# A hybrid encoder layer on one core: its 32 experts from split weight pairs and 64-token halves to float32 throughout, in units of 64 and 32 tokens

## The chip, the cores and the metric

One core of a Trainium2 chip runs the whole layer in one launch. The metric is device time in microseconds (us) of one execution. In what follows PE is TensorE, ACT ScalarE, DVE VectorE, POOL GpSimd and SP SyncE; SP and POOL here mostly issue DMAs.

## The reference

1024 tokens of width 1024 pass a token mixer (mLSTM heads and a spatial gating unit), cross-attention into 256 memory tokens, a mixture of experts, and a final RMSNorm, all in float32. The change lies in the experts:

```python
g_idx    = top_k(softmax(h @ w_rg + b_rg), 1)        # 1 of 4 groups
e_top    = top_k(e_logits of that group, 2)          # 2 of its 8 experts
weights  = p_top * softmax(e_top)
# for each of the 32 experts e, over the tokens that chose it:
y        = (silu(xb @ w_gate[e]) * (xb @ w_up[e])) @ w_down[e]   # 1024 -> 512 -> 1024
out[t]  += weight * y                                 # each token has two experts
x        = x + out;  result = rms_norm(x, g_final)
```

2048 pairs of token and expert fall on 32 experts very unevenly, and which expert gets how many is known only on the device. Every expert's weights are 6 MB.

## The kernel before

The expert stage follows the cross-attention. The hidden rows `h` (normed) and the residual `acc` lie in device memory; a table in device memory (`tab_dram`) holds for every expert its tokens and their weights. The stage walks through blocks, one per expert and a second one for the fullest, in the order of the string `ORDER` (line 42). Four experts are fixed and go first; the others are ranked by their number of tokens on the device (`assign`, line 1254, run in the middle of the first block), and the string says which rank stands where. W is a block of up to 128 tokens, N one of up to 64, T the second block of the fullest expert. Tokens that find no place are done by a loop at the end (line 1487) that runs as often as needed; in the profiled execution it ran no trip.

**Weights.** An expert's weights come as six DMAs of 1 MB on SP's queue (`load`, line 918: four for gate and up, two for down), each into one of `SEATS` = 16 raw buffers of 128 x 2048. `prep_r` issues loads up to the number of free seats; `free` (line 1406) is called when a chunk has been used for the last time and lets it go on. Eleven loads go out before the stage.

**W blocks.** `weights` (line 1156) splits a raw chunk with ACT (cast to the high part, line 108) and DVE (the rest as the low part, line 109) into buffers `wh` and `wl`, four of each; the raw buffer is free once it is split. `mm3` (lines 99 to 102) then does three matmuls in the format f32r for each product, with 128 tokens as stationary and 512 columns moving. `prep_w` (line 1398) runs the splits three chunks ahead of the matmuls (`LA`).

**N and T blocks.** The raw chunk itself is the moving operand, in float32. 64 tokens are the stationary operand, once for the left half and once for the right half of the array's columns, and the two halves get different columns of the weights (`gu_part_n` line 1186, `dn_part_n` line 1225). The trace shows each such float32 matmul as two records. The raw buffer is free when PE has used it. Two N blocks share one gathered tile of 128 tokens.

Each block gathers its tokens from `h` by an indirect DMA on POOL, two blocks ahead (line 1434); PE transposes them (`transpose_x`, line 1414), and SiLU and product are done by ACT and DVE. The down matmuls of block b - 1 run after the gate and up matmuls of block b, and in the midst of the latter `turned` transposes the former's activations.

**Results.** ACT scales each row by its weight, and POOL issues an indirect DMA that adds to `acc`: for a W block 128 whole rows of 4 KB (`store`, line 1236), for an N block 128 half rows of 2 KB (`store_n`, line 1244), since an N block's result lies as left halves on the first 64 partitions and right halves on the others. The final norm reads `acc` afterwards.

```python
LA = 3
for i in range(4):                       # gate and up chunks of block b
    gu_part(...) if wide else gu_part_n(...)
    if not wide: free(b, i)              # narrow: seat free after PE
    done += 1
    prep_w(done + LA)                    # wide: split, seat free after DVE
```

Of the kernel before, what the change touches and what calls it, by code (L numbers as in the profile page):

```python
# [18 lines left out]
P = 128  # L19
# [23 lines left out]
ORDER = "WWWW" + "NNN" + "WN" * 4 + "TWN" + "WN" * 3 + "WWNWWNWNN"  # L43
NS = ORDER.count("N")
SEATS = 16
# [3 lines left out]
def tile_hybrid_encoder(ctx: ExitStack, tc: tile.TileContext,  # L49
# [42 lines left out]
    tab_dram = tc.dram_tile([P * 256, 2], I32, name="tab_dram")  # L92
# [291 lines left out]
    with tpool(name="work1b", bufs=2, side="right") as work, \  # L384
            tpool(name="gmath", bufs=1, side="right") as gm:
        tab0 = gm.tile([P, 256, 2], I32, name="tab0")
        nc.gpsimd.memset(tab0, 0)
        nc.gpsimd.iota(tab0[:, :, 0], pattern=[[0, 256]], base=S, channel_multiplier=1)
        nc.scalar.dma_start(tab_dram.rearrange("(p c) k -> p c k", c=256), tab0)
# [432 lines left out]
    nc.gpsimd.iota(cidx, pattern=[[1, NU]], base=0, channel_multiplier=NU, allow_small_or_imprecise_dtypes=True)  # L822
# [3 lines left out]
    nc.gpsimd.memset(kcol[:, 2:3], 0.0)  # L826
    nc.gpsimd.memset(kcol[64:128, 2:3], 1.0)
# [61 lines left out]
    for k in ORDER:  # L889
        n = sum(b[0] == "W" for b in blocks)  # L890
        if k == "W":
            tw = ORDER[:len(blocks)].count("T")
            blocks.append(("W", ("e", n) if n < FIXED else
                           ("r", 0 if ORDER[len(blocks) - 1] == "T" else n - FIXED + 1 - tw)))
        elif k == "T":
            blocks.append(("N", ("t", 0)))
        else:
            blocks.append(("N", ("r", NL + sum(b[0] == "N" and b[1][0] == "r" for b in blocks))))
# [4 lines left out]
    assert NB == NE + 1 and len(narrow) == NS + 1 and len(narrow) % 2 == 0 and blocks[twin + 1][1] == ("r", 0)  # L903
    seq = []
# [137 lines left out]
    def route_s(t, c, alone=False):  # L1042
# [16 lines left out]
        V.tensor_scalar(bi, bi, 6, None, op0=ALU.logical_shift_right)  # L1059
        bf = small([P, 2], "bf")  # L1060
        V.tensor_copy(bf, bi)
        V.tensor_scalar(pos, pos, 512.0, None, op0=ALU.mult)
        V.scalar_tensor_tensor(pos, eid, 16.0, pos, op0=ALU.mult, op1=ALU.add)
        dst = small([P, 2], "dst", I32)
        V.scalar_tensor_tensor(dst, bf, -32767.0, pos, op0=ALU.mult, op1=ALU.add)
# [73 lines left out]
    with ExitStack() as pa:  # L1139
        rawp[2] = pa.enter_context(tpool(name="raw5", bufs=SEATS - 11))  # L1140
        whp = pa.enter_context(tpool(name="wh7", bufs=4))
        wlp = pa.enter_context(tpool(name="wl7", bufs=4))
        mc = pa.enter_context(tpool(name="mc", bufs=1))
        pgu = pa.enter_context(tpool(name="pgu", bufs=4, space=PSUM))
        xHL = pp.tile([P, KT, P], F32R, name="xH"), pp.tile([P, KT, P], F32R, name="xL")
        ybuf = [pp.tile([P, KT, P], F32R, name=n).rearrange("p a b -> p (a b)").bitcast(F32) for n in ("xH", "xL")]
        xgs += [pp.tile([P, D], F32, name="x1t"), mc.tile([P, D], F32, name="xg")]
        sgt = mc.tile([P, 512], F32, name="sg")
        mHL = mc.tile([P, 4, P], F32R, name="mH"), mc.tile([P, 4, P], F32R, name="mL")
        xTn = mc.tile([P, KT, P], F32, name="xTn")  # L1150
        sgn = sgt[:, 0:256]
        mTn = mc.tile([P, 2, P], F32, name="mTn")
        cnts = {"g": 0, "y": 0}
        acc2 = acc.rearrange("s (h d) -> (s h) d", h=2)

        def weights(r):
            hl = []
            for k in range(2):
                h = whp.tile([P, 1024], F32R, name="wh")
                l = wlp.tile([P, 1024], F32R, name="wl")  # L1160
                split(h, l, r[:, k * 1024:(k + 1) * 1024])
                hl.append((h.rearrange("p (b c) -> p b c", b=2), l.rearrange("p (b c) -> p b c", b=2)))
            return hl
# [4 lines left out]

        def xpose(xg):
            return transposed(xg, trt, xHL)  # L1170

        def xpose_n(xg):
            for g in range(2):
                tp = trt()
# [30 lines left out]
        def mpose(sg):  # L1205
            tp = trt()
            for j in range(4):
                nc.tensor.transpose(tp[:, j], sg[:, j * P:(j + 1) * P], ident)
# [376 lines left out]
```

## Time and profile before

| | us |
|---|---|
| median of 3 runs (lowest, highest) | 1385.25 (1385.24, 1386.29) |
| the profiled execution, whole | 1385.45 |
| the profiled execution, span from first to last instruction | 1383.7 |
| first weight load issued in the expert stage | 774.2 |
| first matmul of an expert | 803.3 |
| end of the last matmul of an expert | 1350.2 |
| final norm, to the end | 1383.7 |

The mean granted TensorE clock was 0.971 of full speed. The page gives busy times per engine over the whole span; a stage has its own mix, so the stretches of the expert stage are read apart. "DMA share" is the mean busy share of the core's 16 DMA engines; a busy engine is no bound unless something waits for it.

### The profile page before, as it was taken

What the parts mean: (1) busy time and instruction counts of PE and PEld (TensorE: products, weight loads), DVE (VectorE), ACT (ScalarE), POOL (GpSimd) and SP (SyncE); (2) the same over time, 40 slices, a digit from 0 to 9 for tenths busy, and PEclk for the clock granted to TensorE, in tenths of its full rate; (3) what the DMA queues carried; (4) which work ended last, traced back from release to release, by engine and by line L of the source; (5) the groups of instructions that cost most, each with busy time, mean ns of one, the idle gap of its engine ahead of it and who ended that gap; (6) DMA issues with size and microseconds to landing.
All of it is one profiled execution on the core that took longest, in us unless ns stands there. A gap on an engine that the chain in (4) does not pass through costs nothing. (4 is left out here: it accounts for less than half of the span.)

```text
span 1383.7 us, 18356 instructions
## 1 busy us (share of the span) xinstructions
PE 1271.4 (92%) x6505; PEld 970.5 (70%) x6505; DVE 793.1 (57%) x1532; ACT 612.9 (44%) x1043; POOL 188.3 (14%) x283
## 2 busy tenths in 40 slices
PE   6899999999897899999999679999999999999980
PEld 6899888888886788888888557655555555566530
DVE  5643465883477765753467668645546454667512
ACT  7632343331474442653222248545446454556522
POOL 2000100000021111110133221112111111100012
PEclk9999999999999999999999879999999999999995
DMA  8820122311798652543963568999999999999967
GB/s 317 267 74 1 36 80 84 92 38 42 236 310 283 215 187 100 199 141 108 338 248 112 213 223 313 388 399 402 399 393 395 392 377 391 378 386 379 384 230 265
DMA packets 86750, 339.53 MB, mean 245 GB/s; under 512 B 12008, under 2 KB 24488, under 8 KB 62081
## 3 DMA queue, kind: packets, MB, share of 16 engines
q1 hardware_dynamic: 72672, 304.53, 59.0%
q0 software_dynamic: 11536, 26.31, 6.6%
q10 hardware_dynamic: 2448, 7.51, 1.4%
q8 instruction: 52, 0.85, 0.3%
q14 instruction: 42, 0.34, 0.1%
HBM read 297.06 MB, written 50.67 MB: 251 GB/s over the span
## 5 line engine op out<-in xcount | busy, mean ns | idle before, releaser
L109 DVE TENSOR_TENSOR wl<-wraw,wh 128x1024 fp32r<-128x1024 f32 (+2 forms) x276 | 325.2, 1210 | 118.2 <-ACT wh L108 106.5
L108 ACT CAST wh<-wraw 128x1024 fp32r<-128x1024 f32 (+2 forms) x276 | 277.7, 1037 | 97.4 <-PE mm L101 29.8
L1191 PE MATMUL gu<-wraw,xTn 128*64 128x512 f32 x512 | 118.2, 598 | 0.5 <-DMA wraw<-in_w_gu_dram 0.5
L101 PE MATMUL gu<-wl,xH 128*128 128x512 f32 x272 | 109.4, 402 | 1.3 <-DVE wl L109 1.1
L102 PE MATMUL gu<-wh,xL 128*128 128x512 f32 x272 | 107.6, 396 | 0.0
L100 PE MATMUL gu<-wh,xH 128*128 128x512 f32 x272 | 99.3, 405 | 2.4 <-ACT wh L108 1.7
L100 PE MATMUL mm<-hH,wh 128*128 128x512 f32 x256 | 100.3, 392 | 0.8 <-ACT wh L108 0.8
L101 PE MATMUL mm<-hL,wh 128*128 128x512 f32 x256 | 100.2, 391 | 0.0
L102 PE MATMUL mm<-hH,wl 128*128 128x512 f32 x256 | 100.0, 391 | 0.0
L1191 PEld LDWEIGHTS gu<-wraw,xTn 128*64 128x64 f32 x512 | 34.2, 136 | 63.8 <-issue 59.7
L108 ACT CAST xH<-tp 128x512 fp32r<-128x512 f32 x64 | 35.4, 589 | 67.7 <-PE tp L738 67.4
L101 PEld LDWEIGHTS gu<-wl,xH 128*128 128x128 f32 x272 | 52.2, 192 | 16.9 <-DVE wl L109 5.7
L100 PEld LDWEIGHTS gu<-wh,xH 128*128 128x128 f32 x272 | 51.9, 191 | 17.2 <-ACT wh L108 4.4
L101 PE MATMUL mm<-wl,hH 128*128 128x384 f32 (+2 forms) x192 | 61.7, 321 | 0.0
L102 PE MATMUL mm<-wh,hL 128*128 128x384 f32 (+2 forms) x192 | 61.6, 321 | 0.0
L100 PE MATMUL mm<-wh,hH 128*128 128x384 f32 (+2 forms) x192 | 61.3, 319 | 0.0
L1228 PE MATMUL y<-wraw,mTn 128*64 128x512 f32 x256 | 60.2, 602 | 1.1 <-ACT mTn L1216 1.1
L101 PE MATMUL y<-wl,mH 128*128 128x512 f32 x136 | 56.3, 414 | 5.2 <-DVE wl L109 5.2
L102 PEld LDWEIGHTS gu<-wh,xL 128*128 128x128 f32 x272 | 51.9, 191 | 11.4 <-DVE xL L109 0.2
L109 DVE TENSOR_TENSOR xL<-tp,xH 128x512 fp32r<-128x512 f32 x64 | 42.7, 685 | 23.7 <-ACT xH L108 23.5
L100 PEld LDWEIGHTS mm<-hH,wh 128*128 128x128 f32 x256 | 48.1, 188 | 10.7 <-ACT wh L108 1.1
L102 PEld LDWEIGHTS mm<-hH,wl 128*128 128x128 f32 x256 | 48.1, 188 | 10.2 <-issue 0.2
(418 smaller groups left out, 2730.5 us busy)
## 6 DMA issues: line engine op xcount, KB each, us to landing
wraw<-in_w_gu_dram SPq DMA_DIRECT2D x128, 1024.0 KB, 22.5
wraw<-in_w_dn_dram SPq DMA_DIRECT2D x64, 1024.0 KB, 23.3
wraw<-in_w_kv_dram SPq DMA_DIRECT2D x16, 512.0 KB, 5.2
xt<-in_x_dram SPq DMA_DIRECT2D x16, 512.0 KB, 5.8
wraw<-in_w_cm_dram SPq DMA_DIRECT2D x16, 512.0 KB, 3.7
x1t<-x_dram SPq DMA_DIRECT2D x16, 512.0 KB, 3.9
wraw<-in_w_tm_dram SPq DMA_DIRECT2D x8, 520.0 KB, 5.3
wraw<-in_w_qT_dram SPq DMA_DIRECT2D x8, 512.0 KB, 7.1
```

The source lines that it names most:

```text
L100: nc.tensor.matmul(o, ah, bh, start=first, stop=False)
L101: nc.tensor.matmul(o, ah, bl, start=False, stop=False)
L102: nc.tensor.matmul(o, al, bh, start=False, stop=last)
L108: nc.scalar.copy(h, r)
L109: nc.vector.tensor_tensor(l, r, f32(h), op=ALU.subtract)
L1191: nc.tensor.matmul(ps[q * 64:q * 64 + 64].rearrange("p (b c) -> p b c", b=2), xT[:, kt, hf * 64:hf * 64 + 64], r4[:, k, :, q * 256:q * 256 ...
L1228: nc.tensor.matmul(ps[q * 64:q * 64 + 64], mT[:, k, i * 64:i * 64 + 64], r[:, k * 1024 + q * 512:k * 1024 + q * 512 + 512], start=i == 0 a ...
```

## The change

All blocks run in float32 from the raw chunks; `weights`, `prep_w`, the buffers `wh` and `wl` and the three-matmul products of the experts are gone. `SEATS` is 20, the four more in the space of those buffers, and every raw buffer is free when PE has used it. The string has new letters: A (15 blocks) is a unit of 64 tokens on column halves, as in N, and a unit of 32 tokens on column quarters: the 32 are stationary four times, and each quarter of the array's columns gets its own 256 columns of the chunk. B (2 blocks) is two units of 64. N and T (16) stay units of 64. `turn` lets the two units of a block swap places from chunk to chunk. Results leave as whole rows for all blocks: ACT copies a 64-unit's two halves (64 x 512 each), DVE a second unit's halves or quarters, onto one tile, DVE scales that tile's rows, and one indirect DMA adds 64, 96 or 128 rows. The table of tokens is cut into units of 32 instead of 64; the rows of the fullest expert's second block come by four small DMAs instead of two; the reads of the ranked order stand ahead of each expert's loads, where ten stood together.

```diff
-ORDER = "WWWW" + "NNN" + "WN" * 4 + "TWN" + "WN" * 3 + "WWNWWNWNN"
+ORDER = "AAAA" + "NNN" + "AN" * 4 + "TBN" + "BN" + "AN" * 2 + "AANAANANN"
-SEATS = 16
+SEATS = 20
...
+    def parts(b):
+        return {"A": [(64, 0, 0), (32, 64, 64)], "B": [(64, 0, 0), (64, 64, 64)],
+                "N": [(64, 64 * half_of[b][1] if b in half_of else 0, 0)]}[...]
...
-        whp = pa.enter_context(tpool(name="wh7", bufs=4))
-        wlp = pa.enter_context(tpool(name="wl7", bufs=4))
...
+        def turn(us, i):
+            us = list(enumerate(us))
+            return us[::-1] if i % 2 else us
+
+        def gu_part(pss, us, xT, r, i):
             r4 = r.rearrange("p (a b c) -> p a b c", a=2, b=2)
+            for u, (n, c0, _) in turn(us, i):
+                w = 4 * n
+                for k in range(2):
+                    kt = 2 * i + k
+                    for q in range(P // n):
+                        nc.tensor.matmul(pss[u][q * n:q * n + n].rearrange("p (b c) -> p b c", b=2),
+                                         xT[:, kt, c0:c0 + n], r4[:, k, :, q * w:q * w + w],
+                                         start=kt == 0, stop=kt == KT - 1)
...
+        def store(pss, us, tok, wt):
             cnts["y"] += 1
+            y = ybuf[cnts["y"] % 2]
+            for u, (n, _, o) in enumerate(us):
+                w = 8 * n
+                for q in range(P // n):
+                    (nc.vector.tensor_copy if u else nc.scalar.copy)(y[o:o + n, q * w:q * w + w], pss[u][q * n:q * n + n])
+            n = us[-1][2] + us[-1][0]
+            nc.vector.tensor_scalar(y[0:n], y[0:n], wt[0:n], None, op0=ALU.mult)
+            nc.gpsimd.indirect_dma_start(out=acc, out_offset=bass.IndirectOffsetOnAxis(ap=tok[0:n], axis=0),
+                                         in_=y[0:n], in_offset=None, bounds_check=S - 1, oob_is_err=False,
+                                         compute_op=ALU.add)
...
                 for i in range(4):
-                    if wide:
-                        gu_part(ps, xx[b], ws[b, i], i)
-                    else:
-                        gu_part_n(ps, xx[b], half_of[b][1], ws[b, i], i)
-                    if not wide:
-                        free(b, i)
-                    done += 1
-                    prep_w(done + LA)
+                    gu_part(ps, us, xx[b], raw(b, i), i)
+                    free(b, i)
```

SP's order at the start of the expert stage, before: five loads (`DMAHW` and `PE` are the semaphores of earlier DMAs and of PE), then six that wait for the splits on ACT and DVE, then the reads of the ranked order.

```order
L920 DMA wraw<-in_w_gu_dram 128x2048 [waits DMAHW1_49,PE_49]
L920 DMA wraw<-in_w_gu_dram 128x2048
L920 DMA wraw<-in_w_gu_dram 128x2048 [waits DMAHW5_49,PE_49]
L922 DMA wraw<-in_w_dn_dram 128x2048 [waits DMAHW6_49]
L922 DMA wraw<-in_w_dn_dram 128x2048 [waits DMAHW7_49]
L920 DMA wraw<-in_w_gu_dram 128x2048 [waits DMAHW0_49,DVE_49,Activation_49]
L920 DMA wraw<-in_w_gu_dram 128x2048 [waits DMAHW1_49,DVE_49,Activation_49]
L920 DMA wraw<-in_w_gu_dram 128x2048 [waits DMAHW2_49,DVE_49]
L920 DMA wraw<-in_w_gu_dram 128x2048 [waits DMAHW3_49,DVE_49]
L922 DMA wraw<-in_w_dn_dram 128x2048 [waits DMAHW4_49,DVE_49]
L922 DMA wraw<-in_w_dn_dram 128x2048 [waits DMAHW5_49,DVE_49]
L1373 TENSOR_LOAD perm [waits DVE_49]
```

The same place with the change, from the first load of the stage on: nine loads that wait for earlier DMAs or for PE of the stage before, then two that wait for PE's use of the first chunks, and then the reads, one ahead of an expert's loads.

```order
L926 DMA wraw<-in_w_gu_dram 128x2048 [waits DMAHW3_49,PE_49]
L926 DMA wraw<-in_w_gu_dram 128x2048 [waits DMAHW4_49]
L926 DMA wraw<-in_w_gu_dram 128x2048 [waits DMAHW5_49,PE_49]
L928 DMA wraw<-in_w_dn_dram 128x2048 [waits DMAHW6_49]
L928 DMA wraw<-in_w_dn_dram 128x2048 [waits DMAHW7_49]
L926 DMA wraw<-in_w_gu_dram 128x2048 [waits DMAHW0_49]
L926 DMA wraw<-in_w_gu_dram 128x2048 [waits DMAHW1_49,PE_49]
L926 DMA wraw<-in_w_gu_dram 128x2048 [waits DMAHW2_49]
L926 DMA wraw<-in_w_gu_dram 128x2048 [waits DMAHW3_49]
L928 DMA wraw<-in_w_dn_dram 128x2048 [waits DMAHW4_49,PE_49]
L928 DMA wraw<-in_w_dn_dram 128x2048 [waits DMAHW5_49,PE_49]
L1349 TENSOR_LOAD perm [waits DVE_49]
```

What moved: the waits for DVE and ACT are gone from the loads, four more loads stand ahead of the first one that needs a used chunk, and that one now waits for PE.

PE's order in the gate and up part of a wide block, before (`gu` is the result in PSUM, `xH` and `xL` the halves of the tokens, `sg` the activations of the block before):

```order
L101 MATMUL gu<-wl,xH 128x512
L102 MATMUL gu<-wh,xL 128x512
L1208 MATMUL tp<-ident,sg 128x128 x4
L100 MATMUL gu<-wh,xH 128x512
L101 MATMUL gu<-wl,xH 128x512
L102 MATMUL gu<-wh,xL 128x512
L100 MATMUL gu<-wh,xH 128x512
```

A block of the kind A with the change (`gh`, `yh` are results of the 64-unit, `gq`, `yq` of the 32-unit; `wraw` is the moving operand, the shape is that of one result: tokens x columns):

```order
L1189 MATMUL gh<-wraw,xH 64x512 x4
L1189 MATMUL gq<-wraw,xH 32x256 x16
L1189 MATMUL gh<-wraw,xH 64x512 x4
L1207 MATMUL tp<-ident,sg 128x128 x3
L1189 MATMUL gh<-wraw,xH 64x512 x4
L1189 MATMUL gq<-wraw,xH 32x256 x16
L1189 MATMUL gh<-wraw,xH 64x512 x4
L1165 MATMUL tp<-ident,xg 128x128 x8
L1222 MATMUL yh<-wraw,mT_7588 64x512 x4
L1222 MATMUL yq<-wraw,mT_7589 32x256 x16
L1222 MATMUL yh<-wraw,mT_7588 64x512 x4
L1189 MATMUL gh<-wraw,xL 64x512 x4
```

What moved: three records of 128 x 512 for each product have become 64 x 512 in pairs and 32 x 256 in fours, and the two units alternate with a change of shape in the middle of each chunk.

ACT's last instructions of the stage, before (`mTn` are the last activations, `xH` and `xL` here the tiles of results):

```order
L1239 ACTIVATE xL<-y,wtw 128x512 x2
L1201 ACTIVATE sg<-gu 128x256
L1246 ACTIVATE xH<-y,wtn 128x512
L1216 COPY mTn<-tp 128x256
L1246 ACTIVATE xL<-y,wtn 128x512
```

The same with the change:

```order
L1198 ACTIVATE sg<-gh 128x256
L1231 COPY xH<-yh 64x512 x2
L1210 COPY mT_7588<-tp 128x256
L1464 DMA gfb<-in_g_final_dram 128x1024
L1231 COPY xL<-yh 64x512 x2
```

What moved: the last result takes two copies on ACT where there was one scaling, and a scaling of 64 x 1024 on DVE follows them.

## Rows read from the trace of the kernel before

**Rows 1.** The page's part 1: busy time of each engine, its share of the span, instructions.
```profile
PE 1271.4 (92%) x6505; PEld 970.5 (70%) x6505; DVE 793.1 (57%) x1532; ACT 612.9 (44%) x1043; POOL 188.3 (14%) x283
```

**Rows 2.** The expert stage cut into stretches (windows view): start and end in us, length, then busy us and instructions of PE, PEld, DVE, ACT and POOL, the granted TensorE clock, the share of the 16 DMA engines' time, GB/s.
```profile
774.00:790.00 16.00, 8.65 (x51) 6.63 (x50) 11.23 (x55) 6.75 (x13) 1.65 (x4) 0.84 0.91 341
790.00:810.00 20.00, 10.61 (x43) 8.53 (x42) 13.75 (x42) 4.80 (x8) 8.24 (x9) 0.62 0.51 176
810.00:820.00 10.00, 5.88 (x27) 4.51 (x26) 9.08 (x24) 7.02 (x7) 2.62 (x2) 0.95 0.97 364
820.00:850.00 30.00, 28.65 (x125) 23.30 (x126) 22.72 (x43) 19.04 (x23) 3.96 (x3) 0.85 0.68 237
...
880.00:1325.00 445.00, 423.73 (x1903) 249.16 (x1902) 232.19 (x240) 223.82 (x289) 63.30 (x45) 0.99 1.01 390
1325.00:1330.00 5.00, 4.96 (x12) 3.39 (x11) 4.09 (x4) 2.26 (x3) 0.00 (x0) 0.50 1.00 416
1330.00:1340.00 10.00, 10.00 (x45) 4.64 (x44) 0.00 (x0) 1.27 (x2) 1.56 (x1) 0.95 0.42 146
1340.00:1346.00 6.00, 4.46 (x22) 1.26 (x18) 0.42 (x1) 0.89 (x2) 0.00 (x0) 1.00 0.15 46
```

**Rows 3.** The DMA view of the stretch 880 to 1325 us: the two queues with packets, MB and share of the 16 engines (q1 holds the weight loads, q0 gathers and stores of tokens), and the weight loads issued there, KB each, median us from issue to landing.
```profile
q1 hardware_dynamic: 21973, 160.03, 89.1%
q0 software_dynamic: 6624, 13.22, 12.1%
...
wraw<-in_w_gu_dram SPq DMA_DIRECT2D x100, 1024.0 KB, 23.3
wraw<-in_w_dn_dram SPq DMA_DIRECT2D x54, 1024.0 KB, 23.6
```

**Rows 4.** What SP, the engine that issues the weight loads, waited for from 770 us on (waits view): line and what released it, us in total, times, longest us.
```profile
SPq L920 <- DMA wraw<-in_w_gu_dram: 113.4, 48, 4.7
SPq L920 <- DMA wraw<-in_w_dn_dram: 101.1, 42, 4.3
...
SPq L920 <- DVE wl L109: 53.3, 17, 14.4
```

**Rows 5.** SP's timeline around the start of the expert stage and at its last loads: start, length of the piece, line, operation, count.
```profile
774.24 6.04 SPq L920 DMA_DIRECT2D wraw<-in_w_gu_dram  x3
780.33 0.90 SPq L922 DMA_DIRECT2D wraw<-in_w_dn_dram  x2
795.65 17.13 SPq L920 DMA_DIRECT2D wraw<-in_w_gu_dram  x4
815.51 4.54 SPq L922 DMA_DIRECT2D wraw<-in_w_dn_dram  x2
...
1315.98 8.87 SPq L922 DMA_DIRECT2D wraw<-in_w_dn_dram  x4
```

**Rows 6.** PE's timeline (PE is the matmuls, PEld the loading of their weights): the first expert matmul, the gap at the ordering of experts, eight transposes and the 24 matmul records of a wide block's down part that follow them, a transpose between matmuls of 64 columns, two waits near the end, a 64-token gate/up part and the last down part. In brackets the idle time ahead and what ended it.
```profile
803.31 0.79 PE L100 MATMUL gu<-wh,xH 128*128 128x512 f32 x1
...
820.17 0.26 PE L1275 MATMUL tp<-MT,kcol 32*1 32x32 f32 x2 [4.29 <-DVE t L1340]
...
838.98 1.03 PE L738 MATMUL tp<-ident,xg 128*128 128x128 f32 x8
839.77 0.48 PE L100 MATMUL y<-wh,mH 128*128 128x512 f32 x1
...
845.31 0.39 PE L100 MATMUL gu<-wh,xH 128*128 128x512 f32 x1
...
1312.00 0.33 PE L1208 MATMUL tp<-ident,sg 128*128 128x128 f32 x1
...
1312.26 1.94 PE L1228 MATMUL y<-wraw,mTn 128*64 128x512 f32 x8
...
1322.63 0.44 PE L1215 MATMUL tp<-ident,sg 128*128 128x128 f32 x2 [0.94 <-DVE sg L1202]
...
1324.48 1.22 PE L100 MATMUL y<-wh,mH 128*128 128x512 f32 x2 [1.41 <-ACT wh L108]
...
1333.35 7.09 PE L1191 MATMUL gu<-wraw,xTn 128*64 128x512 f32 x32
...
1333.83 0.14 PEld L1191 LDWEIGHTS gu<-wraw,xTn 128*64 128x64 f32 x2 [0.29 <-issue]
...
1346.50 3.65 PE L1228 MATMUL y<-wraw,mTn 128*64 128x512 f32 x16 [1.10 <-ACT mTn L1216]
```

**Rows 7.** The timeline after the last matmul: ACT's scaling of the last result, POOL's issue of the last store.
```profile
1350.25 0.69 ACT L1246 ACTIVATE xL<-y,wtn 128x512 f32<-128x512 f32 x1 [3.80 <-issue]
1351.82 1.56 POOL L1247 DMA_INDIRECT acc<-xL,tk  x1 [3.80 <-ACTq L1486]
```

**Rows 8.** Groups of instructions from 700 us on, shapes apart (lines view): busy us and mean ns of one, then idle time ahead.
```profile
L109 DVE TENSOR_TENSOR wl<-wraw,wh 128x1024 fp32r<-128x1024 f32 x204 | 241.3, 1222 | 73.0 <-ACT wh L108 70.2 <-DMA wraw<-in_w_gu_dram 0.3
...
L1191 PE MATMUL gu<-wraw,xTn 128*64 128x512 f32 x512 | 118.2, 598 | 0.5 <-DMA wraw<-in_w_gu_dram 0.5
...
L1523 DVE SCALAR_TENSOR_TENSOR ft<-ft,frs,gfb 128x1024 f32<-128x1024 f32 x8 | 10.3, 1284 | 28.0 <-DMA ft<-acc 22.7 <-POOL frs L97 5.3
```

**Rows 9.** The DMA view of 957.4 to 962.4 us, in which one whole-row store runs: the software queue's packets, MB and share of the 16 engines.
```profile
q0 software_dynamic: 138, 0.45, 45.3%
```

**Rows 10.** The DMA view of 913.7 to 918.2 us, in which one half-row store runs: the same columns.
```profile
q0 software_dynamic: 144, 0.26, 31.6%
```

More of the change, by code (lines that the diff above doesn't have):

```diff
@@ L888, in tile_hybrid_encoder @@
     blocks = []
[L889 to L896, printed above, removed]
+    rank = {"A": 2, "N": NL}
+    for n, k in enumerate(ORDER):
+        if n < FIXED:
+            blocks.append((k, ("e", n)))
+        elif k in rank:
+            blocks.append((k, ("r", rank[k])))
+            rank[k] += 1
         else:
-            blocks.append(("N", ("r", NL + sum(b[0] == "N" and b[1][0] == "r" for b in blocks))))
+            blocks.append(("N", ("t", 0)) if k == "T" else (k, ("r", int(ORDER[n - 1] != "T"))))
     NB = len(blocks)
@@ L1244, in store_n @@
-        def store_n(ps, tok2, wt2):
-            y = next_y()[:, 0:512]
-            nc.scalar.activation(y, ps, AF.Copy, scale=wt2)
-            nc.gpsimd.indirect_dma_start(out=acc2, out_offset=bass.IndirectOffsetOnAxis(ap=tok2, axis=0),
-                                         in_=y, in_offset=None, bounds_check=2 * S - 1, oob_is_err=False,
-                                         compute_op=ALU.add)
-        def ps2(pool, name):
-            return [pool.tile([P, 512], F32, name=name) for _ in range(2)]
+                (nc.scalar.copy if g else nc.vector.tensor_copy)(xT[:, g * 4:g * 4 + 4], tp)
@@ new lines, in silu_mul, with mpose @@
+        def silu_mul(pss, us):
+            sg = []
+            for u, (n, _, _) in enumerate(us):
+                w = 4 * n
+                t = sgt[:, u * 256:u * 256 + w]
+                nc.scalar.activation(t, pss[u][:, 0:w], AF.Silu)
+                nc.vector.tensor_tensor(t, t, pss[u][:, w:2 * w], op=ALU.mult)
+                sg.append(t)
+            return sg
+        def mpose(sg, us):
+            tp = trt()
+            for u, (n, _, _) in enumerate(us):
+                for j in range(n // 32):
+                    nc.tensor.transpose(tp[:, 2 * u + j], sg[u][:, j * P:(j + 1) * P], ident)
+            for u, (n, _, _) in enumerate(us):
+                m = n // 32
+                (nc.vector.tensor_copy if u else nc.scalar.copy)(mTs[u][:, 0:m], tp[:, 2 * u:2 * u + m])
+            return mTs
@@ new lines, in dn_part @@
+        def dn_part(pss, us, mm, r, i):
+            for u, (n, _, _) in turn(us, i):
+                w = 8 * n
+                for k in range(2):
+                    if n == 64:
+                        lh = mm[u][:, k, i * 64:i * 64 + 64]
+                    else:
+                        lh = mm[u][:, 0, (2 * i + k) * 32:(2 * i + k) * 32 + 32]
+                    for q in range(P // n):
+                        nc.tensor.matmul(pss[u][q * n:q * n + n], lh, r[:, k * 1024 + q * w:k * 1024 + q * w + w],
+                                         start=i == 0 and k == 0, stop=i == 1 and k == 1)
@@ L1467, in tile_hybrid_encoder @@
                         assign()
[L1468 removed]
+                sgs[b] = silu_mul(ps, us)
                 if b + 1 < NB:
@@ L1471, in tile_hybrid_encoder @@
             else:
[L1472 removed]
+                mm = mpose(sgs.pop(b - 1), parts(b - 1))
             if b > 0:
[L1474 to L1475 removed]
+                us = parts(b - 1)
+                ys = y_tiles(us)
                 for i in range(2):
[L1477 to L1482 removed]
+                    dn_part(ys, us, mm, raw(b - 1, 4 + i), i)
+                    free(b - 1, 4 + i)
+                store(ys, us, *rows_of(b - 1))
         lr = pl["lr"]
```

275 lines of the change are left out of this document (93 added, 182 removed).

## The prediction

> **What bounds the kernel now.** The profiled execution took 1385.45 us: a span of 1383.7 us and 1.75 us around it; the median of the runs is 1385.25, so the sum below is made against 1385.45. Two runs of this kernel can be told apart from about 0.2% (2.8 us) on.
>
> I read the page's first part, then the stretches of the expert stage, then SP's waits. PE is busy 92% of the span [rows 1], which looks like a PE-bound kernel. The stretches say otherwise for the stage that changes: from 880 to 1325 us the DMA engines are at 1.01 of their time, moving 390 GB/s, while PE has 21 us to spare [rows 2]. The weight queue alone takes 89.1% and the software queue (gathers and stores of tokens) 12.1% [rows 3]; 160.03 MB are 152.6 loads of 1 MB in 445 us, so a load costs 2.92 us of time, 2.6 us of the engines by itself (0.891 × 445 / 152.6). SP, which issues the loads, waits mostly on earlier loads [rows 4]. DMA is the bound from 880 to about 1330 us, and what a change in PE, ACT or DVE gives there is nothing unless it lets a transfer start earlier.
>
> It is not bound by DMA at the start. From 774 us (the last weights that need no split) to 850 us the share is 0.91, 0.51, 0.97, 0.68 [rows 2]: 1.4 + 9.8 + 0.3 + 9.6 = 21 us in which the engines stand idle. SP's timeline shows why: five loads leave by 781.2, the next at 795.65, and these four take 17 us to issue [rows 5], each held until DVE has split an earlier chunk (53.3 us of waiting in all [rows 4]). At the end the last load is issued at 1324.85 (1315.98 + 8.87 [rows 5]) and the engines fall to 0.42 and 0.15 [rows 2]: the last bytes land near 1346, PE ends at 1350.15 (1346.50 + 3.65 [rows 6]), and a tail of 33.5 us follows: ACT's scaling, the last store [rows 7], the final norm.
>
> **PE, part by part.** Seventeen blocks of three split matmuls go. One costs 72 pairs of load and matmul at 5.54 / 24 = 0.231 us (839.77 to 845.31 [rows 6]), 16.6 us, with transposes 18.1. A 64-token block in float32 stays as it is: 7.09 us for 8 steps of the contraction and 3.65 for 4 (0.43 per two records, 0.86 per step), 10.3 us, and 11.5 with 6 transposes of 0.10 (0.79 / 8) and four changes of shape at 0.15 (1312.00 to 1312.26 less one transpose) [rows 6].
>
> Fifteen blocks become a 64-unit and a 32-unit. The 32-unit has no row. Nearest is the 64-unit: its two halves load their weights together (two loads in 0.14 us) and a pair of records 512 columns wide takes 0.43, although one record lasts 598 ns [rows 6, 8]. One f32 transpose takes 0.10 us for 128 columns, so a lone record 512 wide would take about 0.4: the two halves run side by side. If four quarters do so too, a step costs half, 0.43 us (256 columns); if the array takes no more than the two streams a row has shown, 0.86. I take 0.43, since the pair shows no loss at all from going side by side, and keep 0.86. Block: 10.3 + 12 × 0.43 + 11 transposes (1.2) + 10 changes of shape (1.5) = 18.2 us. Two blocks of 64 + 64 cost 22.5 (20.6, transposes and changes of shape). Sum: 15 × 18.2 + 2 × 22.5 + 16 × 11.5 + 5 for the gap while the experts are put in order (4.29 us [rows 6]) = 507 us. From 804.5 (803.31 [rows 6], a copy later) PE's work ends at 1311.5: PE has about 25 us in hand against the last landing, so this term is 0 on the path. The cover is gone when a 32-unit step costs more than 0.57 (180 steps × 0.14 = 25 us).
>
> The change of shape, at 150 places, is priced at 0.15 us by the row. The Trainium skill, "TensorEngine Tiling (Array Packing)", Key Properties, says that a change of tiling mode drains the array. The row shows such a change (64 to 128 columns) for 0.15 us, far less than the 598 ns that a record lasts, so a drain is there at most in part. By the row the 150 changes come to 22 us of PE, hidden; drained in full they would come to 90, and that is a rival below.
>
> **Splits.** The ACT casts and the DVE subtractions (204 × 1.22 us [rows 8]) go. They ran beside DMA: 0 on the path by themselves. What they did on the path is hold SP at the start, and that is in the next term.
>
> **Weight buffers, 20 for 16, freed by PE.** SP's order now holds nine loads before the first that waits for this stage, where there were five. By the semaphores in that order, six leave at once, and three behind the stores of the last tile's residual and hidden rows, near 792 to 795. Nine loads are 23 us of engine time: DMA runs from 774.5 to about 801. Then buffers are full until PE has used its first chunk near 807 (two chunk halves at 0.86 and 0.43 per step, 2.6 us): 5.5 us idle. After that a chunk comes free every 18.2 / 6 = 3.0 us against 2.9 for a load, so the queue stays fed; I add 4.3 us for the gap at the ordering of experts and 3 for the transposes of the first tiles. With the first 1.4 us that is about 14 idle where there were 21: **−7 us**, and between 0 (nothing recovered) and −13 (the loads fill all but 8 us). What stands behind the waiting loads on SP are the reads of the experts' order, now one ahead of each expert's loads, and the four small loads of the doubled expert's rows in place of two: under 1 us each, hidden by 20 full buffers. If that cover were gone, each would cost its wait, some 2 us.
>
> **Stores.** An accumulate of whole rows: 45.3% of 5 us for 0.45 MB, 110 rows, 20.6 ns a row [rows 9]. Half rows: 31.6% of 4.5 us for 128 halves, 22.2 ns a whole row [rows 10]. By the counts of the reference's inputs about 770 of the 2048 rows lie in 64-token blocks and change form: **−1.2 us** of a DMA-bound stretch. The gathers stay. By the same counts no expert has more tokens than its places before or after (92 for 96, 64 for 64), so the extra loop makes no trip.
>
> **End.** The order of work after the last landing is the same two chunks of 64-token matmuls. PE waits for loads there, and its clock can fall: after two waits of 0.94 and 1.41 us the granted clock was 0.50 in 1325 to 1330 [rows 2, 6], that is 1.2 GHz. A last chunk is 1.7 us at full and 3.4 at half clock, where PE now ends 4.2 after the last bytes: −2.5 to +2, and I take **−0.8**. Behind it the last store has two ACT copies where there was one (+0.65, by 0.69 [rows 7]) and a DVE scaling of 64 × 1024, between 0.6 and 1.28 us by the row of a 1024-wide DVE operation [rows 8]: **+1.7**. Nothing covers that; the store then has its old length.
>
> **Sum.** −7 − 1.2 − 0.8 + 1.7 = −7.3 against 1385.45: **1378 us**. PE, ACT and DVE drop by far more, and none of it shows. With the bounds (idle −11 to −3, end −2 to +2) the forecast's own range is 1371 to 1384.
>
> **Rivals.**
> *Slower: the quarters run two at a time.* A 32-unit step then costs 0.86, a block 23.4 us, PE ends at 1311.5 + 180 × 0.43 = 1389 and the kernel at 1389 + 33.5 + 1.7 + 1.75 = **1426**. It decides from 0.57 on and is slower than before from 0.64 on. For it: no row has the array take columns faster than two 512-wide records in 0.43 us. Against: the two halves lose nothing to each other, and loads go in pairs in 0.14. Chance 0.12.
> *Slower: each change of shape empties the array in full*, 0.6 us (a record's length [rows 8]) instead of 0.15: 150 × 0.45 = 68 us more PE, which ends at 1380, the kernel at about **1417**. The row of 0.15 speaks against it. The rule of "TensorEngine Tiling (Array Packing)" above would have it so. Chance 0.04.
> *The idle at the start isn't won back.* The three late loads, the gather behind nine loads and PE's own late start (its first tokens now share DMA with four more loads) leave the engines about 20 us idle; with the other terms **1384**, no change. This is the case in which the change doesn't do what its buffers are for. For it: the loads behind the stores. Chance 0.14.
> *More is won.* The engines end unevenly: from 1330 to 1346 they are at 0.42 and 0.15, some 11 us of their time [rows 2]. If loads queued deeper come out evener by 6 us and the idle falls to 8, it is **1366**. Against: the mix of transfers is nearly the old one. Chance 0.08.
>
> **How the numbers follow.** The forecast has 0.62. Faster by over 0.2% (under 1382.5) are nearly all of it, the last rival and a fifth of the third: 0.71. Within 0.2% (to 1388): the rest of the third and a little of the forecast: 0.13. Slower: the first two, 0.16. The range must reach past the third rival and its spread, and to a 32-unit step a little over the point where PE takes the end (0.67 per step is 1391), and down to the fourth: 1364 to 1392. It leaves out the two slower cases at their full price, 0.16.
>
> **What would show it.** Right: DMA near 1.0 from 807 to the end, idle before 850 near 14 us; records of 32 × 256 in fours, a set each 0.21 us; PE idle on loads in the last 30 us, its clock partly at 0.50; ACT and DVE under half their time. Wrong: PE without a gap until the end and DMA waiting on PE (the first rival); sets of four at 0.43; gaps of 0.4 us and more at each change of shape; first matmul later than 806, or the nine loads issued over 20 us and more.

## The result and the profile after

The changed kernel takes **1360.42 us** (median of 4 runs, 1359.35 to 1365.1) against 1385.24 before: 0.9836 of it, 95% interval 0.98 to 0.9871, 24.8 us less. In a later repeat (x_again), for which 1359 to 1365 was expected, it took 1363.28 against 1384.68, ratio 0.9838 (0.9812 to 0.9864). The forecast was 1378, the range began at 1364: the direction was right, the gain more than three times the forecast.

The page's part 1 of the changed kernel, which answers to [rows 1]:

```profile
PE 1263.0 (93%) x7616; PEld 839.4 (62%) x7616; DVE 587.4 (43%) x1418; ACT 408.6 (30%) x855; POOL 182.4 (13%) x281
```

The expert stage in stretches (columns as in [rows 2]), of the changed kernel:

```profile
774.00:790.00 16.00, 6.52 (x37) 5.30 (x35) 11.00 (x65) 1.78 (x6) 2.06 (x4) 0.65 1.00 397
790.00:810.00 20.00, 11.17 (x64) 5.06 (x66) 2.32 (x16) 1.87 (x2) 9.16 (x10) 0.60 0.61 219
810.00:820.00 10.00, 9.48 (x68) 3.90 (x66) 4.85 (x32) 1.25 (x3) 0.92 (x1) 1.00 0.85 294
820.00:850.00 30.00, 30.00 (x260) 11.61 (x256) 4.93 (x12) 3.82 (x9) 2.62 (x3) 1.00 0.96 339
880.00:1300.00 420.00, 411.69 (x2695) 149.68 (x2693) 76.80 (x157) 66.84 (x142) 58.26 (x44) 1.00 1.01 398
1300.00:1310.00 10.00, 10.00 (x72) 3.47 (x70) 2.44 (x5) 1.53 (x3) 1.42 (x1) 1.00 0.64 261
1310.00:1320.00 10.00, 7.39 (x36) 2.29 (x34) 1.17 (x2) 1.92 (x4) 0.49 (x1) 1.00 0.49 159
```

Two things are to be seen. The hole between 790 and 850 is smaller: 0.61, 0.85 and 0.96 where there were 0.51, 0.97 and 0.68. And in the long stretch the engines' share is 1.01 as before, but in that same share they move 398 GB/s and not 390. The share alone would say that nothing had changed there.

The DMA view of the stretch 880 to 1300 us, which answers to [rows 3]; the last rows are stores of whole rows, with their count and the median us from issue to landing:

```profile
q1 hardware_dynamic: 21107, 153.74, 88.8%
q0 software_dynamic: 5167, 12.92, 12.3%
...
acc<-xL,tkr POOLq DMA_INDIRECT x13, 7.8
acc<-xH,tkr POOLq DMA_INDIRECT x12, 8.9
```

153.74 MB are 146.6 loads in 420 us: 2.865 us of time for a load where it was 2.92. Over the 181 loads of the stage that would be 10 us.

SP's timeline at the start and at the last loads, against [rows 5]:

```profile
769.32 5.76 SPq L926 DMA_DIRECT2D wraw<-in_w_gu_dram  x3
775.13 0.90 SPq L928 DMA_DIRECT2D wraw<-in_w_dn_dram  x2
776.07 14.88 SPq L926 DMA_DIRECT2D wraw<-in_w_gu_dram  x4
806.84 3.03 SPq L928 DMA_DIRECT2D wraw<-in_w_dn_dram  x2
...
1288.56 7.80 SPq L928 DMA_DIRECT2D wraw<-in_w_dn_dram  x4
```

Nine loads leave by 790.95, where five left by 781.23. PE's timeline of the changed kernel: the first matmuls, a block of the kind A from 819.33 to 837.53, and the last part. Records of 128*32 are the 32-token unit; in brackets the idle time ahead.

```profile
799.90 1.97 PE L1165 MATMUL tp<-ident,x1t 128*128 128x128 f32 x8 [8.61 <-DMA x1t<-h,tokt]
801.80 3.68 PE L1189 MATMUL gh<-wraw,xL 128*64 128x512 f32 x8
...
819.33 1.94 PE L1189 MATMUL gh<-wraw,xH 128*64 128x512 f32 x8 [0.52 <-DVE xH L1166]
821.20 1.93 PE L1189 MATMUL gq<-wraw,xH 128*32 128x256 f32 x32
823.06 1.94 PE L1189 MATMUL gh<-wraw,xH 128*64 128x512 f32 x8
...
831.01 1.09 PE L1165 MATMUL tp<-ident,xg 128*128 128x128 f32 x8
832.03 1.94 PE L1222 MATMUL yh<-wraw,mT 128*64 128x512 f32 x8
833.90 1.93 PE L1222 MATMUL yq<-wraw,mT 128*32 128x256 f32 x32
835.76 1.94 PE L1222 MATMUL yh<-wraw,mT 128*64 128x512 f32 x8
837.53 1.89 PE L1189 MATMUL gh<-wraw,xL 128*64 128x512 f32 x8
...
1313.58 3.65 PE L1222 MATMUL yh<-wraw,mT 128*64 128x512 f32 x16
1318.91 3.65 PE L1222 MATMUL yh<-wraw,mT 128*64 128x512 f32 x16 [1.67 <-ACT mT L1210]
```

What PE waited for from 770 us on (us in total, times, longest):

```profile
PE tp L1165 <- DMA x1t<-h,tokt: 8.6, 1, 8.6
PE tp L1207 <- DVE sg L1199: 8.5, 9, 0.9
...
PE yh L1222 <- ACT mT L1210: 1.7, 1, 1.7
```

No matmul of the experts waits for a weight load. The last weights land at 1318.3, PE's last matmul ends at 1322.56, 4.2 us later (3.9 before). Behind it, against [rows 7]:

```profile
1322.61 1.17 ACT L1231 COPY xL<-yh 64x512 f32<-64x512 f32 x2 [3.75 <-PE yh L1222]
1323.82 0.75 DVE L1233 TENSOR_SCALAR xL<-xL,wtr 64x1024 f32<-64x1024 f32 x1 [4.58 <-ACTq L1438]
1324.84 1.40 POOL L1234 DMA_INDIRECT acc<-xL,tkr  x1 [3.93 <-DVEq L1438]
```

**Where the 26.1 us of the span (1383.7 to 1357.6) came from**, in the two profiled executions; the last landing is the end of the last weight packet in the trace:

| piece | before | after | change | forecast |
|---|---|---|---|---|
| span's start to the stage's first load | 774.2 | 769.3 | −4.9 | 0 |
| first load to last landing | 572.1 | 549.0 | −23.1 | −8.2 |
| last landing to the span's end | 37.4 | 39.3 | +1.9 | +0.9 |

The first piece is scatter: it lies ahead of what the change touches, and it varied from 769.3 to 776.8 over the profiles of all kernels here, 773.1 in the repeat of the changed one. In the second, the engines' idle time in the first 76 us fell from 21.4 to 11.6 us (−9.8, counted from the packets as a mean of 16 engines; 10.6 in the repeat). The other 13.3 us are in transfers, where the forecast had 1.2. What they are is what the experiments had to find.

### The profile page after: what moved, and what is told of

Read it like the earlier page. It is cut to its first block, busy times and chain, and to the rows that moved or that the text cites. A ratio compares the mean times of both kernels' runs of the same rounds, so it can differ in the third digit from the quotient of the medians.

```text
span 1357.6 us, 20099 instructions
## 1 busy us (share of the span) xinstructions
PE 1263.0 (93%) x7616; PEld 839.4 (62%) x7616; DVE 587.4 (43%) x1418; ACT 408.6 (30%) x855; POOL 182.4 (13%) x281
## 5 line engine op out<-in xcount | busy, mean ns | idle before, releaser
L1222 PE MATMUL yh<-wraw,mT 128*64 128x512 f32 x560 | 133.6, 600 | 1.7 <-ACT mT L1210 1.7
L1189 PE MATMUL gh<-wraw,xTn 128*64 128x512 f32 x512 | 118.8, 596 | 0.0
L111 DVE TENSOR_TENSOR wl<-wraw,wh 128x1024 fp32r<-128x1024 f32 (+2 forms) x72 | 83.1, 1166 | 42.4 <-ACT wh L110 33.5
L110 ACT CAST wh<-wraw 128x1024 fp32r<-128x1024 f32 (+2 forms) x72 | 71.4, 1002 | 44.0 <-PE mm L103 29.8
L1189 PE MATMUL gh<-wraw,xL 128*64 128x512 f32 x320 | 82.8, 612 | 0.0
L1189 PE MATMUL gh<-wraw,xH 128*64 128x512 f32 x288 | 67.3, 600 | 0.5 <-DVE xH L1166 0.5
L102 PE MATMUL pc<-wh,yh 128*128 128x512 f32 x128 | 50.9, 402 | 3.3 <-ACT yh L110 3.2
L102 PE MATMUL mm<-vH,xH 128*128 128x512 f32 x128 | 53.8, 420 | 0.0
L103 PE MATMUL pc<-wl,yh 128*128 128x512 f32 x128 | 50.9, 399 | 1.6 <-DVE wl L111 1.6
L102 PE MATMUL mm<-aH,xH 128*128 128x512 f32 x128 | 51.1, 399 | 0.0
```

Source lines behind the costliest of these rows:

```text
L102: nc.tensor.matmul(o, ah, bh, start=first, stop=False)
L103: nc.tensor.matmul(o, ah, bl, start=False, stop=False)
L110: nc.scalar.copy(h, r)
L111: nc.vector.tensor_tensor(l, r, f32(h), op=ALU.subtract)
L1189: nc.tensor.matmul(pss[u][q * n:q * n + n].rearrange("p (b c) -> p b c", b=2), xT[:, kt, c0:c0 + n], r4[:, k, :, q * w:q * w + w], start=k ...
L1222: nc.tensor.matmul(pss[u][q * n:q * n + n], lh, r[:, k * 1024 + q * w:k * 1024 + q * w + w], start=i == 0 and k == 0, stop=i == 1 and k == 1)
```

## Experiments

The theories go by letters in the expectations. **U** (uneven): a store is shared out among the 16 DMA engines by the rows that it *names*, also where its rows point out of bounds and are skipped; a load is spread over all 16 and is done with the slowest; so a store costs the rows named, not the rows written. (In the expectation of x_skipped U stands for a narrower form, by which only written rows cost.) **S** (split): ACT's casts and DVE's subtractions slowed the loads by their own traffic. **H** (half rows): the 2 KB packets of the half-row stores slowed them. **R**: each skipped row costs an engine about as much as a written one. **B** (bytes): what counts is what is written. "Landing" is the time from the stage's first load to its last landing (before 572.1, changed 549.0, repeat 548.1). The ratios are to the kernel before, which took 1385.1, 1384.7 and 1383.7 in the three groups of runs.

**x_store128**: the changed kernel, with its stores of the blocks A and N naming 128 rows, 1440 more in all. The rows added are out of bounds: as many rows are written as without the edit. (It also clears the two result tiles once.)

```
 nc.vector.tensor_scalar(y[0:n], y[0:n], wt[0:n], None, op0=ALU.mult)
+n = P if wide else n          # wide: blocks A and N
 nc.gpsimd.indirect_dma_start(out=acc, ... ap=tok[0:n] ..., in_=y[0:n],
```

> The changed kernel, but the accumulating store of every A and N block (not of T) names 128 rows instead of 96 or 64; the added rows carry no token and are skipped. Theory U (the slowest of the 16 DMA engines sets the end of the loads; a store's rows lie on the engines in contiguous runs, so the engines with the first rows get more the longer the list of rows is): one row costs an engine about 0.33 us (20.6 ns x 16), the first engines get 2 more rows in 15 A blocks and 4 more in 15 N blocks, 90 x 0.33 = 30 us, of which some 2 us are hidden behind PE: 1380 to 1390 us. Theory S (the loads were slowed by the traffic of the splits on ACT and DVE) and theory H (by half-row packets of 2 KB): skipped rows cost nothing, 1359 to 1363.

Measured: 1389.41 (1385.64 to 1391.85), ratio 1.0028; landing 577.9. The whole gain is gone, by an edit that leaves PE, splits and buffers as in the changed kernel. Its DMA view of 880 to 1290 us:

```profile
q1 hardware_dynamic: 19407, 141.36, 87.5%
q0 software_dynamic: 6043, 12.34, 12.1%
...
acc<-xL,tkr POOLq DMA_INDIRECT x12, 10.5
acc<-xH,tkr POOLq DMA_INDIRECT x11, 10.7
```

Its long stretch, and two of PE's waits:

```profile
880.00:1300.00 420.00, 398.18 (x2571) 143.27 (x2571) 75.00 (x153) 64.55 (x137) 59.89 (x44) 1.00 1.00 376
```

```profile
PE yh L1222 <- DMA wraw<-in_w_dn_dram: 9.1, 10, 2.1
...
PE gh L1189 <- DMA wraw<-in_w_gu_dram: 7.0, 10, 1.4
```

The software queue has the same share, the stores land 2 to 3 us later (10.5 and 10.7 for 7.8 and 8.9), and the DMA engines, at 1.00, move 376 GB/s instead of 398. PE waits for loads again. As U expected; S and H expected nothing of it.

The packets of a single store show what U says. The store of the first N block writes 64 rows (0.26 MB) in both kernels. Here is the software queue in two stretches of 2.6 us from the store's first packet on, first in the changed kernel (905.7 to 908.3 and on to 910.9), which names 64 rows:

```profile
q0 software_dynamic: 71, 0.26, 50.5%
q0 software_dynamic: 9, 0.00, 0.2%
```

and in x_store128 (908.9 to 911.5 and on to 914.1), which names 128:

```profile
q0 software_dynamic: 105, 0.16, 31.3%
q0 software_dynamic: 39, 0.11, 20.7%
```

The same 64 rows take twice as long when 128 are named. So it is for the other stores of whole rows between 870 and 1300 us: from the first written row's start to the last one's are 2.3 us when 64 rows are named and 3.7 when 96 (medians in the changed kernel), and 4.8 when 128 (x_store128; 4.9 in the kernel before). In the kernel before it was 4.4 for a store that wrote 46 rows and 4.6 for one that wrote 110. A skipped row is a packet of 8 bytes in the trace, of some 9 ns; a written one takes 327 ns.

**x_written128**: the same, with the skipped rows written too (to 128 spare rows behind `acc`).

```
+n = P if wide else n
-bounds_check=S - 1
+bounds_check=S + P - 1 if wide else S - 1     # acc has S + P rows
```

> The kernel with 128 named rows in every A, B and N store (1389 us with the rows skipped), all of them written, 2055 rows more than the changed kernel writes. Theory U: the slowest engine already wrote 8 rows in each store, so nothing is added: 1386 to 1393. Theory B: 2055 x 20.6 ns = 42 us more of DMA than the kernel with skipped rows: over 1420.

Measured: 1387.13 (1384.04 to 1388.3), no more than with the rows skipped. Its DMA view of 880 to 1290 us:

```profile
q1 hardware_dynamic: 19307, 140.60, 82.3%
q0 software_dynamic: 6123, 18.82, 19.6%
```

Half as many bytes again in the software queue, its share up from 12.1 to 19.6%, and no time: most of that comes out of the weight queue's share (87.5 to 82.3%). Weight packets seem to have been waiting inside that share: of those that start between 880 and 1280 us the median takes 309 ns in both runs, but 485 took over 500 ns in x_store128 and 38 here (303 in the kernel before, 170 in the changed one). **x_written** did it to the changed kernel as it is, whose A, B and N stores skip 615 rows (`bounds_check` and `acc` as above, no wider store):

> The changed kernel, but the 615 rows that its A, B and N stores name and skip are written too, to 128 spare rows behind the result. Theory U (a store gives each of the 16 DMA engines a sixteenth of its named rows; where rows are skipped, some engines get their full share and others less, and the loads, which are spread over all 16, wait for the engine with the most): the engines that wrote less now write as much as the first ones, the slowest engine does nothing more: 1359 to 1364. Theory B (the sum of what is written decides): 615 x 20.6 ns = 12.7 us more DMA, 2 hidden: 1370 to 1375.

Measured: 1364.81 (1361.19 to 1366.27), against 1360.4 and 1363.3 without: a little over U's range, below B's. B is refuted by both, U holds.

**x_before96**: the kernel before, with the stores of its blocks W (those of the two fullest experts aside) naming 96 of their 128 rows. No row that is written is left out.

```
-def store(ps, tok, wt):
+def store(ps, tok, wt, n=P):           # n = 96 for W
-    ... ap=tok ..., in_=y,
+    ... ap=tok[0:n] ..., in_=y[0:n],
```

> The kernel before, but the stores of its W blocks (not the two that hold the fullest experts) name 96 rows instead of 128; no token lies in the others. Theory U: 15 blocks x 2 rows x 0.33 = 10 us less on the first engines, 1375 to 1378. Theories S and H: no change, 1384 to 1387.

Measured: 1380.61 (1378.71 to 1384.17), ratio 0.9968 (0.9949 to 0.9988); landing 560.1, so 12.0 us off the DMA's time, of which 4.5 reach the end, less than U expected: PE, with its splits and three-fold matmuls, then ends 11.1 us behind the last landing, where it was 3.9. S and H expected no change.

**x_nosmall**: the changed kernel without the 32-token units (`"A": [(64, 0, 0)]` in `parts`): the results of those tokens are left out, the A stores name 64 rows, not 96.

> The changed kernel without the 32-token units: the A blocks compute and store their first 64 tokens only, so the rows of the others are left out. PE has 15 x 5.2 = 77 us less to do and is out of the way. Theory U: the slowest engine writes 2 rows less in 15 stores, 10 us, and the kernel ends some 2 us behind the last load: 1346 to 1352. If the loads' end does not hang on the named rows, only the 2 us by which PE ended behind the last load go: 1356 to 1361. If PE were still the bound: no room for that, since 77 us are gone.

Measured: 1344.54 (1343.85 to 1346.87), a little under U's range; landing 532.7, PE ends 2.7 us after. PE has some 15 × 7 us less to do and waits for loads:

```profile
PE gh L1189 <- DMA wraw<-in_w_gu_dram: 28.0, 36, 1.7
```

So fewer named rows still pay when PE is out of the way; of the 16.3 us, 4.0 are less idle time at the start (7.6 for 11.6). In the runs in which PE waits for loads up to the end (this one, x_store128) it ends 2.7 to 2.9 us behind the last landing. In the changed kernel, where it waits for none, it ends 4.2 behind: there (3.8 in the repeat) PE's own work is the bound by some 1 to 1.5 us, with DMA right behind it.

**x_skipped**: the changed kernel with one more store in each block, of 64 rows that are all out of bounds.

> The changed kernel with one more accumulating store behind each block's own, of 64 rows whose indices are all out of bounds: nothing is written and no byte moves. Theory R (a row that a store names costs the DMA engines about 20.6 ns, or 0.33 us of one of them, whether it is written or skipped; it replaces theory U, since dealing the rows evenly changed nothing): 33 x 64 x 20.6 ns = 43 us more of DMA, some 2 hidden: 1398 to 1406. Theory U (only written rows cost, and the engine with the most of them decides) and theory H: 1360 to 1364.

Measured: 1382.49 (1380.5 to 1389.33), 20 us slower, where R expected 1398 to 1406 and the narrower U 1360 to 1364. But the landing is 544.9, no later than without: these stores cost DMA nothing. The time is elsewhere: PE ends 563.5 us after the first load where it was 553.2, and behind it come 44.5 us, not 35.1, since the last extra store stands in the final chain. Half of PE's ten shows as waits for DVE (13.6 for 8.5); the rest is open.

```profile
PE tp L1210 <- DVE sg L1202: 13.6, 9, 4.0
```

R falls, though the time alone would have looked like half a hit. It also limits U: a store in which *no* row is written has no engine with a full share to wait for.

**x_dummy**: the changed kernel with the 204 casts and subtractions put back on dummy data (19 buffers).

> The changed kernel with 19 buffers and, after each chunk of an A or B block, two casts on ACT and two subtractions on DVE of 128 x 1024 into a tile that nothing reads (204 of each, as many as the kernel before had). Theory S: the weight loads take some 9 us of engine time more again (474 us in the stage of the kernel before, 465 in the changed one), 1366 to 1371. Theories U and H: the loads stay at 465; at most 3 us more for PE waiting behind the added work on ACT and DVE, 1360 to 1364.

Measured: 1414.89 (1413.19 to 1415.98), beyond every expectation. PE waits 42.9 us, at 14 places, for DVE:

```profile
PE tp L1216 <- DVE sg L1208: 42.9, 14, 8.5
```

The added work sits ahead of the block's own on ACT and DVE and holds PE, so this run can't tell what it does to the loads. S stays unproven, and isn't needed: x_store128 gives the gain back without any split, and without a half row.

**x_seats16**: the changed kernel with 16 buffers (`SEATS = 16`).

> The changed kernel with 16 weight buffers instead of 20. Theory of the buffers (they fill the idle DMA time at the start): four loads fewer go out ahead of PE's first chunk, 4 x 2.6 = 10 us of DMA time are idle, the loads end some 10 us later and PE waits for them: 1367 to 1373. Rival (the nine loads only push the table's scatters and the first gather back, so that PE starts 3 to 4 us late, and DMA has time enough): 1356 to 1361.

Measured: 1367.07 (1365.54 to 1372.73), 3.8 to 6.7 us slower than with 20. Landing 554.9. SP's longest wait for PE, the one for the first chunk, takes 25.1 us where it took 15.8 (the last number of each row, first of x_seats16, then of the changed kernel):

```profile
SPq L926 <- PE gq L1189: 37.1, 5, 25.1
```

```profile
SPq L928 <- PE gq L1189: 24.6, 5, 15.8
```

PE itself starts earlier with 16 (27.7 us after the first load for 32.5): four loads fewer stand ahead of its first gather. The four more buffers are worth some 5 us net.

**x_before_even**: the kernel before, with the tokens of an expert dealt over the 128 rows (token j to row 8·(j mod 16) + j div 16, in place of row j).

> The kernel before, but the tokens of the ranked experts are dealt to the partitions in turn (token j to partition 8 (j mod 16) + j div 16, in N blocks within each half likewise), so that the rows of a store or a gather lie evenly on the DMA engines; the same rows, bytes and packets. Theory U: the first engines lose about 11 x 2.8 x 0.33 + 15 x 1.9 x 0.18 us of stores and 7 us of gathers, 22 us in all, of which PE may hide a few: 1363 to 1372. Theories S and H: no change, 1384 to 1387.

Measured: 1385.01 (1381.76 to 1389.92), ratio 0.9995. No change; landing 573.1. Here U missed: if each engine took eight neighbouring rows, this would have evened out the written ones. The trace shows that it didn't: the written rows of the dealt stores take as long as before (4.4 us for the 70 rows at 1289 us, 4.9 for the same store of the kernel before). Which engine takes which row is therefore not what I had assumed. A dealing in runs of four rows, rows 0 to 63 to one half of the engines and 64 to 127 to the other, would fit the packets: of 46 written rows (the store at 888.5 us of the kernel before) 34 start in the first four steps of 0.64 us and 12 in the later ones. Under it the new order leaves eight written rows on half of the engines, as the old one did. No run tests it.

**x_g96**: the changed kernel, with gathers of the A blocks of 96 rows in place of 128 (the rows left out were skipped ones). **x_early96**: the same, and the first gather is moved ahead of two table stores on POOL's queue.

> The changed kernel with gathers of 96 rows for the A blocks and nothing else. Theory U: the slowest engine reads 2 rows less in 15 gathers, 15 x 2 x 0.16 = 5 us less DMA, which PE hides: 1358 to 1362. If the 10 us that the loads took longer in the kernel with the early gather came from these gathers and not from its order: 1368 to 1372.

> The changed kernel with the gather of the first tokens ahead of the last but one tile's two table scatters on POOL (they follow the first three gathers), and with gathers of 96 rows instead of 128 for the A blocks. The trace of the changed kernel has PE without a wait for a weight load from its first matmul on, so it is bound by PE's start: the gather can leave near 790.5 (when the hidden rows have landed) instead of 794.3, PE starts 3 to 4 us sooner, and DMA, which ended some 2 us ahead of PE, follows by the 15 x 32 rows no longer named (480 x 10 ns = 5 us by a gather's row price): 1355 to 1358 against the 1360 to 1363 of the changed kernel. If DMA is the bound after all and skipped gather rows cost nothing: 1359 to 1363.

Measured: 1370.89 (1369.43 to 1374.23) and 1370.04 (1367.58 to 1372.88): both some 8 us slower than the changed kernel; landings 558.1 and 559.1. U had x_g96 gain or stay. The moved gather got away earlier, but its rows landed later (first of x_early96, then of the changed kernel):

```profile
796.31 1.09 POOL L1087 DMA_INDIRECT x1t<-h,tokt  x1 [12.03 <-DMA wraw<-in_w_gu_dram]
```

```profile
794.27 1.07 POOL L1081 DMA_INDIRECT x1t<-h,tokt  x1 [0.30 <-issue]
```

It starts 22.1 us after the stage's first load (774.25), where it was 25.0 (769.32). But its rows then run among the nine loads: the DMA share is 0.99 from 798 to 804 us, and PE's first transposes come 32.9 us after the first load instead of 30.6. (The profile puts its wait of 12.03 us down to a weight load, which the gather doesn't read; a releaser is inferred, and no run tells whether it was the hidden rows instead.) Why gathers that name fewer rows, and read as many, cost 9 us of DMA time is open. The packets of x_g96 show where they sit: between 880 and 1280 us 972 weight packets take 350 to 500 ns, where 66 did, nearly all of them while a gather runs, and many rows of the gathers take over 175 ns, where the usual row takes 160. No version tried is faster than the changed kernel with all of its work in it.

## Why the prediction was wrong

**The bound was read rightly.** DMA bounded the stage of the kernel before: ACT's busy time fell by a third and DVE's by a quarter, and the time followed the landings. PE's hardly fell (1271.4 to 1263.0 us), against "PE, ACT and DVE drop by far more".

**The step that failed is "Stores: −1.2".** It priced what changes in the *rows written* (some 770 whole rows instead of halves), from the mean share of 16 engines in [rows 9, 10]. The change also cuts the rows *named*: before, every store names 128 rows (17 whole, 16 by halves); after, 96, 128 and 64 (15 × 96 + 2 × 128 + 16 × 64 = 2720). At the same 20.6 and 22.2 ns a row this is 2176 × 0.0206 + 2048 × 0.0111 = 67.6 us before and 2720 × 0.0206 = 56.0 after: **−11.6 us**, ten times the term. The runs bear the price out: 480 named rows less took 12.0 us off the landing (x_before96, 9.9 by the price), 480 less again 16 (x_nosmall, in which written rows go too), 1440 more added 28.9 (x_store128, 29.7), and writing the named rows or not made no difference. [rows 9] were a store of 110 written rows of 128 named, so the price came out nearly right and only the count was wrong. The diff showed it (`tok[0:n]`), and I read it as no more than a form of the row.

What misled is the mean share. At 1.01 in both kernels, it includes packets that take far longer than the rest: 303 weight packets of over 500 ns before, 170 after, beside a median of 309 in both. That these wait on engines that could go on, while the load's slowest engine works off its rows of a store, is inferred; that they all but vanish when every engine has its full share to write (38 in x_written128) speaks for it. By queue this shows as weight time: the weights' packets took 474 us of a mean engine from first load to PE's end before, and 465 after, for the same bytes.

**The idle at the start was −9.8 where −7 was forecast**, inside its own bounds (0 to −13). The mechanism is as told: nine loads instead of five, then a hole until PE frees chunks (0.61 of 790 to 810). The transposes and the ordering of experts, for which 7 us were added, didn't hold the loads: the 4.29 us gap of [rows 6] is gone, since the matmuls of the next unit now run in it. With 16 buffers (x_seats16) the idle is 16.6 us, so 5.0 of the 9.8 hang on the four buffers and 4.8 came without them, with the splits gone that held SP.

**PE's prices held; its slack did not.** A 32-unit step costs 0.47 us with its share of a change of shape (1.86 for four steps: 821.20 to 823.06), a block of the kind A 18.2 (819.33 to 837.53), as forecast. So the quarters do run four at a time, and the first rival falls. So does the second: two steps of 64 columns, four of 32 and two of 64 stand back to back, and the first two groups take 0.14 to 0.15 us more each than at 0.86 and 0.43 a step. The rule of the Trainium skill, "TensorEngine Tiling (Array Packing)", Key Properties, that a change of tiling mode drains the array, shows here as no more than that; the measurement decides. The total was 13.8 us low: from 801.80 to 1322.56 PE takes 520.8, not 507. The nine waits for `sg` (8.5 us, [rows 6] shows one of 0.94) were left out, and 1.7 us of the first eight matmuls (3.68 for 1.94) went to a granted clock that was still at 0.50 (1.2 GHz) after 8.6 us of waiting; 3.6 us are not accounted for. With that, and landings 19 us earlier than forecast, "25 us in hand" became none. It cost little: PE ends 4.2 us after the last landing, 3.9 before.

**The end** was +1.9 for +0.9. The tail behind PE's last matmul grew by 1.5 us, near the forecast +1.7, but only 0.6 of it is the copies and the scaling (1.17 and 0.75 for 0.69): the last store leaves 2.3 us after PE's end where it left 1.7 after it, since ahead of the old store there was a gap of 0.9. The other 0.9 lies behind the store's issue, and its cause is open. That the sum came out near is luck. The gain of 0.8 at the last chunk didn't come (+0.4); PE no longer waits for loads there, so its clock stayed at 1.00 up to the last 1.67 us wait.

**"More is won", the rival at 1366,** had the right side and a small part of the reason. The engines do end a little more evenly: they still take 22 us from the last issue (1296.36) to the last landing, but stand idle for 8.2 us of it (8.0 in the repeat) where it was 11.0, a gain of 2.8 and not 6. With 128 rows named (x_store128) it is 10.9 again. The rest of the gain lies between start and end, where this rival had none.

**What the price of a named row does not explain:** −9.8 − 11.6 are −21.4 of the −23.1 before the last landing. The rest, 1.7 us, is left over.

## What to carry to other kernels

When loads share the engines, count an indirect store that writes anything by the rows that it names, not by those that it writes: cut the row list to what the block can hold. Where the mean DMA share is already 1.0, look at GB/s and at the time from a store's issue to its landing in the same stretch, since the share does not fall when packets wait (1.00 at 376 GB/s in x_store128). And when one engine is the bound and another has slack, work out the slack again for every case of the forecast, the better ones too.

## What the runs showed of the hardware

- Skipped rows are not free beside written ones: 1440 of them added to stores took 28.9 us of the stage (x_store128), and writing them took nothing more (1387 for 1389). The same 64 written rows take twice as long when 128 rows are named. Alone in a store they cost DMA nothing (landing 544.9 for 549.0, x_skipped).
- Four float32 units of 32 columns by 256 run side by side on PE: a step of the contraction takes 0.47 us so, half of what it takes as two units of 64 by 512 (1.86 us for four steps, 1.87 for two, a change of shape included).
- Gathers that name 96 rows instead of 128, with as many bytes, took 9 us more (x_g96). It is open why, and no run tests which rows go to which engine.
- The start of the stage moved between 769.3 and 776.8 us with kernels that hardly differ ahead of it; differences of 5 us and less need several runs.
